# The block inverse of an RWKV-7 recurrence in one stretch of VectorE, and its 64-row products on quarters of the TensorE array

## The chip, the core and the metric

The kernel runs on one core of a Trainium2 chip. The metric is the device time of one launch in microseconds. Engines: PE is TensorE (matrix products, its weight loads are shown as PEld), DVE is VectorE, ACT is ScalarE, POOL is GpSimd, SP issues most DMAs. Each engine works its own instructions off in order; semaphores tie them together.

## What is computed

The kernel is one launch of three layers over 512 positions of width 1024: an attention layer, an RWKV-7 layer and a layer with two state-space branches, with the feed-forward parts. Only the recurrence of the RWKV-7 layer is touched. For each of 16 heads (64 channels) and both directions it computes, position after position,

```
sa    = state @ (-kk_t)
state = state * w_t + outer(sa, kk_t * a_t) + outer(v_t, k_t)
out_t = state @ r_t
```

then a group norm over each head, a bonus term, a gate, and the sum over the two directions. All of it is in 32-bit floats.

## The kernel before, in words

Positions are cut into 8 chunks of 64, and the 16 heads into 8 pairs of heads. In a chunk the recurrence is solved with matrix products: the scores of the chunk's keys against its keys give a strictly triangular 64x64 matrix for each head and direction, which has to be inverted (plus the identity); with the inverse, a chunk becomes one affine step of the 64x64 state. The two directions lie side by side: direction 0 on one half of the 128 partitions, direction 1 on the other.

Function `rwkv` does this with eleven generators, each a stream of work over the 8 pairs: `values` (the product that gives v), `front` and two `half` (keys, decays), `scores`, `inverse`, `early`, `merge`, `mid`, `chain` and `post`.

- `scores` (four groups of two chunks for a pair) makes the masked scores, tile `at`, and stores the 32x32 diagonal blocks to DRAM (`nd_s`). There are nine `at` buffers: by its condition a group waits until the chain has done the steps of the group nine places earlier.
- `inverse` (L1694) loads the diagonal blocks in another layout, 16x16 sub-blocks with one matrix in each partition, into X and, for direction 1, XL. XL has the pool tag `v1`, which a tile of `merge` has too, with one buffer. After the copy of XL into X (L1704) it runs 14 steps of two VectorE operations, a product into `xt` and a sum into X. Each needs the one before it, and after each stands a `yield`. Then it sets the diagonal (L1715) and stores X to DRAM (`xd_s`).
- `merge` (L1741) loads the 16x16 inverses (`yd`), transposes them into `zd`, and puts the 64x64 inverses together with 32x32 products on TensorE: tile `tt`.
- `early` (L1719) fills one partition half of the tiles `uv` (one for each direction) with v and clears the other half with a memset on POOL.
- `mid` (L1811) takes each group of two chunks through three sets of products. `ahead` copies `ar` through TensorE with the identity (four instructions in the profile) and multiplies `at` by `uv` (eight), twice. Then `tt` multiplies the result (`ax`), ACT copies it out: the first halves into `ta`, the others into the halves of `uv` that were zero. Then `ta` multiplies `at`, and DVE adds `ar` and the identity to make the transfer matrix `m`. `tas` are two fixed `ta` tiles, cleared once, in which each direction's half of the partitions is filled for its own slot; the other half stays zero, so that products over 128 rows give the 64-row result.
- `chain` (L1873) takes the state through the 8 chunks with `m` and writes `o`; `post` (L1913) normalises it and stores `y`.

The profile shows two instructions on TensorE for each such product of 32-bit floats. A product's place in the array follows from its operands: its rows from the partitions that it reads, its columns from the partitions that it writes. 128*64 in a row means 128 rows and 64 columns of the array.

The order of the instructions is written when the program is built, by `weave` (L36). Each generator yields the engine and the tiles that its next piece of work needs (or a condition); `weave` keeps a small model of engine times and takes the piece that can start first, by the time at which engine and operands are free, and among equals the one that became ready first. All instructions up to the generator's next `yield` are issued in one go, and each compute engine keeps that order.

Of the kernel before, what the change touches and what calls it, by code (L numbers as in the profile page):

```python
# [24 lines left out]
class Net:  # L25
# [1265 lines left out]
    def rwkv(self, g_pre, mu_p, mu_n, w_r, w_k, w_v, w_o, k_k, k_a, r_k, gn_w, gn_b, w0, w1, w2, a0, a1, a2,  # L1291
# [35 lines left out]
        with ExitStack() as c0:  # L1327
# [110 lines left out]
            with ExitStack() as c1:  # L1438
# [2 lines left out]
                arp, uvp, qp = P1("arp", 2), P1("uvp", 2), P1("qp", 4)  # L1441
                cw = ExitStack()
                self.weights(cw, 2, 2)
                vout = self.pool(cw, "vout")
                late = {}
                pm, pu = P1("pm", 5, space=PSUM), P1("pu", 3, space=PSUM)
                mk = sh.tile([128, 2, 128], F32, name="mk")
# [7 lines left out]
                TT(V, ident2, self.ident[:, 0:64], self.ident[:, 64:128], AD)  # L1455
                zeros = lambda nm, shape: [sh.tile([128] + shape, F32, name=f"{nm}{j}") for j in range(2)]

                tts, ss, tas = zeros("tt", [8, 2, 64]), zeros("ss", [2, 128]), zeros("ta", [2, 2, 2, 64])
                for j, t in enumerate(tts + ss + tas):
                    (V, G)[j % 2].memset(t, 0.0)  # L1460
                bank = lambda: pm.tile([128, 512], F32, name="mb", tag="mb")
                T2 = lambda tag, bufs=2: tp.tile([128, 520], F32, name="tmp", tag=tag, bufs=bufs)
# [44 lines left out]
                def values():  # L1507

                    ws = {}

                    def weight(j):
                        raw = self.wraw.tile([128, 1024], F32, name="raw", tag="raw")
                        nc.sync.dma_start(out=raw.rearrange("p (a b) -> p a b", b=128), in_=w_v[:, rows(j)].rearrange("(k p) c -> p k c", p=128))
                        hi, lo = (self.whl.tile([128, 1024], F32R, name=n, tag=n) for n in ("whi", "wlo"))
                        yield AC, raw
                        ACT(hi, raw, AF.Copy)
                        yield DV, hi
                        TT(V, lo, raw, hi.bitcast(F32), SU)
                        ws[j] = [t.rearrange("p (a b) -> p a b", b=128) for t in (hi, lo)]

                    yield from weight(0)
                    for j in range(KD):
                        if j + 1 < KD:
                            yield from weight(j + 1)
                        b = bank()
                        for k in range(KD):
                            if k % 2 == 0:
                                yield PE, *ws[j]
                            self.mm3(b, (ws[j][0][:, k, :], ws[j][1][:, k, :]), (xv[k][:, 0, :], xv[k][:, 1, :]), k == 0, k == KD - 1)
                        yield AC, b  # L1530
                        t = vout.tile([128, S], F32, name="vo", tag="vo")
                        ACT(t, b, AF.Copy)
                        nc.sync.dma_start(out=rkv_d[2, rows(j), :], in_=t)
                        done["values"] = j + 1
                    cv.close()
                    cw.close()
                    late.update(mp=P1("mp", 2), arp=P1("arl", 1), o=P1("ol", 1), qp=self.pool(c0, "qpl", 5, side="right"))
# [156 lines left out]
                def inverse(p, st):  # L1694

                    yield lambda: done["pre"] > p
                    XL = sh.tile([128, 16, 32], F32, name="XL", tag="v1")
                    for q in range(2):

                        for d in range(2):  # L1700
                            o = slice(64 * d + 32 * q, 64 * d + 32 * q + 32)
                            nc.sync.dma_start(out=flat((X, XL)[d][o])[:, :512 - 16 * q], in_=nd_d[p, 32 * d:32 * d + 32, 528 * q:512 + 512 * q])
                    yield DV, XL
                    V.tensor_copy(out=X[H(1), :, 0:16], in_=XL[H(1), :, 0:16].rearrange("p s t -> p t s"))  # L1704
                    yield DV, X
                    xt = sh.tile([128, 64], F32, name="xt_", tag="xt_")
                    for j in range(1, 15):
                        n = 15 - j
                        t = xt[:, :j * n].rearrange("p (i c) -> p i c", c=n)
                        TT(V, t, X[:, 0:j, j].unsqueeze(2).to_broadcast([128, j, n]),  # L1710
                           X[:, j, j + 1:16].unsqueeze(1).to_broadcast([128, j, n]), M)
                        yield DV, xt
                        TT(V, X[:, 0:j, j + 1:16], X[:, 0:j, j + 1:16], t, AD)
                        yield DV, X
                    V.memset(flat(X)[:, 0:512:33], 1.0)  # L1715
                    nc.sync.dma_start(out=xd_v[p], in_=flat(X))
                    done["inverse"] += 1

                def early(p, st):  # L1719
# [5 lines left out]
                    yield lambda: done["step"] >= 8 * (p - 1)  # L1725
                    uv = [uvp.tile([128, 8, 2, 64], F32, name=f"uv{d}", tag=f"uv{d}") for d in range(2)]
                    st["uv"] = uv
                    for d in range(2):
                        yield PO,
                        G.memset(uv[d][H(d)], 0.0)  # L1730
                    yield PE, v
                    b = bank().rearrange("p (c t) -> p c t", t=128)
                    for c in range(4):
# [77 lines left out]
                def mid(p, st):  # L1811
# [5 lines left out]
                    def ahead(i):  # L1817
                        b = bank().rearrange("p (j h e x) -> p j h e x", j=2, h=2, e=2)
                        at = st["q", i]
                        for j in range(2):  # L1820
                            cs = chunk_of(2 * i + j)
                            for d in range(2):
                                MM(b[H(d), j, :, 0, :], ar[d][:, cs[d], d, :], self.ident.rearrange("p (h x) -> p h x", h=2), True, True)
                            for hp in range(2):
                                for d in range(2):
                                    MM(b[H(d), j, hp, 1, :], at[:, j, hp, 2 * d, H(d)], uv[d][:, cs[d], hp, :], True, True)
                        return b

                    for i in range(4):
# [15 lines left out]
                                for d in range(2):  # L1845
                                    MM(b[H(d), j, hp, :], tt[H(d), 2 * i + j, hp, :], ax[H(d), 2 * j + hp], True, True)
                        yield AC, b
                        ta = tas[i % 2]
                        for d in range(2):
                            ACT(ta[H(d), d], b[H(d), :, :, 0:64], AF.Copy)  # L1850
                        yield AC, b
                        ACT(uv[0][H(0), 2 * i:2 * i + 2], b[H(0), :, :, 64:128], AF.Copy)
                        yield AC, b
                        ACT(uv[1][H(1), 6 - 2 * i:8 - 2 * i][:, ::-1], b[H(1), :, :, 64:128], AF.Copy)
                        yield PE, ta
                        b = bank().rearrange("p (j d x) -> p j d x", j=2, d=2)
                        for j in range(2):
                            for d in range(2):
                                for hp in range(2):
                                    MM(b[H(hp), j, d, :], ta[:, d, j, hp, :], lhs(at[:, j], d, hp), True, True)  # L1860
                        yield DV, b
                        m = mp.tile([128, 2, 2, 128], F32, name="m", tag="m", bufs=3)
                        for d in range(2):
                            cs = slice(6 - 2 * i, 8 - 2 * i) if d else slice(2 * i, 2 * i + 2)
                            r = ar[d][:, cs, 1 - d, :]
                            TT(V, m[:, :, d, H(d)], b[:, :, d, H(d)], r[:, ::-1] if d else r, AD)
                        i4 = lambda t: t.rearrange("p j d x -> p j (d x)")[:, :, 64:192].rearrange("p j (d x) -> p j d x", d=2)
                        TT(V, i4(m), i4(b), ident2.unsqueeze(1).unsqueeze(1).to_broadcast([128, 2, 2, 64]), AD)
                        st["m", i] = m
                        b = nx  # L1870
                    done["mid"] += 1
# [266 lines left out]
```

## Time and profile before

| | us |
|---|---|
| median of 3 runs | 2333.58 (2332.74 to 2334.99) |
| the profiled execution | 2329.99 |
| its span | 2328.2 |
| PE busy, in the span | 2135.0 (92%) |
| DVE busy | 1276.4 (55%) |
| ACT busy | 1077.6 (46%) |
| POOL busy | 85.3 (4%) |

Times in the rows below are in us from the start of the span, durations of a group in the timeline run from the first start to the last end, and means are in ns. `<-` in an operation's name stands between what it writes and what it reads; after an idle time it stands before the operation that ended the wait. The recurrence lies between about 820 and 1340 us.

### The profile page before, as it was taken

To read this page: it belongs to the slowest core of one execution; us is meant where nothing else is said; L and a number is where in the kernel's file an instruction comes from. 1 tells how busy PE (TensorE), PEld (TensorE's weight loads), DVE (VectorE), ACT (ScalarE), POOL (GpSimd) and SP (SyncE) were. 2 spreads that over 40 slices of the span, in tenths; PEclk is the share of its full clock that TensorE was granted. 3 is DMA by queue.
4 is the path that set the end of the run, shared out by engine and by line. 5 is a ranking of instruction groups with operands and counts; after the bars stand their busy time and mean duration, and the time that the engine had idled before them with its cause. 6 is when DMAs were issued, how large, how long until landed. Compare 5 with 4: busy or idle time off the path is not lost. (4 is left out here: it accounts for less than half of the span.)

```text
span 2328.2 us, 40334 instructions
## 1 busy us (share of the span) xinstructions
PE 2135.0 (92%) x16330; PEld 1719.8 (74%) x16330; DVE 1276.4 (55%) x2562; ACT 1077.6 (46%) x1950; POOL 85.3 (4%) x123
## 2 busy tenths in 40 slices
PE   7898999999968788888898689999999999999998
PEld 6777788888856666666676568887787877788877
DVE  4656542333388765667664255387645566633353
ACT  4555353342356554777766544333233444522232
POOL 0000000000000000011100100000000000000000
PEclk9999999999979987989999899999999988899999
DMA  5311233233224233222222343324334544233341
GB/s 173 104 55 54 71 110 92 90 100 100 91 71 121 91 99 80 61 61 57 52 55 46 105 133 109 91 90 144 111 111 142 143 126 119 54 95 90 107 145 55
DMA packets 321028, 221.52 MB, mean 95 GB/s; under 512 B 82414, under 2 KB 274442, under 8 KB 320842
## 3 DMA queue, kind: packets, MB, share of 16 engines
q1 hardware_dynamic: 319402, 213.70, 32.3%
q10 hardware_dynamic: 1440, 5.24, 0.7%
q8 instruction: 129, 2.11, 0.4%
q14 instruction: 57, 0.47, 0.1%
HBM read 187.62 MB, written 27.07 MB: 92 GB/s over the span
## 5 line engine op out<-in xcount | busy, mean ns | idle before, releaser
L160 ACT ACTIVATE whi<-raw 128x1024 fp32r<-128x1024 f32 x220 | 231.1, 1052 | 585.9 <-PE mm L223 297.3
L161 DVE TENSOR_TENSOR wlo<-raw,whi 128x1024 fp32r<-128x1024 f32 x220 | 266.5, 1214 | 368.0 <-ACT whi L160 365.4
L222 PE MATMUL mm<-uth,whi 128*128 128x512 f32 (+1 forms) x1088 | 412.9, 382 | 2.1 <-ACT uth L196 2.1
L223 PE MATMUL mm<-utl,whi 128*128 128x512 f32 (+1 forms) x1088 | 406.6, 374 | 5.5 <-DVE utl L197 5.5
L224 PE MATMUL mm<-uth,wlo 128*128 128x512 f32 (+1 forms) x1088 | 406.6, 374 | 0.0
L223 PEld LDWEIGHTS mm<-utl,whi 128*128 128x128 f32 x1088 | 209.0, 192 | 43.2 <-DVE utl L197 6.7
L222 PEld LDWEIGHTS mm<-uth,whi 128*128 128x128 f32 x1088 | 208.3, 192 | 41.0 <-ACT uth L196 3.5
L224 PEld LDWEIGHTS mm<-uth,wlo 128*128 128x128 f32 x1088 | 208.8, 192 | 37.3 <-issue 1.1
L224 PE MATMUL mm<-whi,hl 128*128 128x512 f32 x512 | 200.6, 394 | 0.0
L222 PE MATMUL mm<-whi,hh 128*128 128x512 f32 x512 | 200.5, 394 | 0.0
L223 PE MATMUL mm<-wlo,hh 128*128 128x512 f32 x512 | 199.9, 393 | 0.0
L224 PEld LDWEIGHTS mm<-whi,hl 128*128 128x128 f32 x512 | 96.3, 188 | 22.0 <-issue 0.2
L223 PEld LDWEIGHTS mm<-wlo,hh 128*128 128x128 f32 x512 | 96.3, 188 | 21.6
L222 PEld LDWEIGHTS mm<-whi,hh 128*128 128x128 f32 x512 | 96.3, 188 | 21.5 <-issue 0.4
L222 PE MATMUL mm<-whi,uth 128*128 128x512 f32 x224 | 88.6, 401 | 8.5 <-ACT whi L160 6.4
L224 PE MATMUL mm<-whi,utl 128*128 128x512 f32 x224 | 88.7, 399 | 0.0
L223 PE MATMUL mm<-wlo,uth 128*128 128x512 f32 x224 | 88.5, 398 | 0.0
L1301 ACT ACTIVATE ss<-cp,wc 64x64 f32<-64x64 f32 x224 | 69.1, 309 | 27.6 <-PE cp L1302 22.7
L282 DVE TENSOR_TENSOR acc<-mm,acc 128x512 f32<-128x512 f32 x48 | 33.0, 688 | 77.6 <-PE mm L224 77.6
L223 PE MATMUL mm<-mx,whi 128*128 128x512 f32 x160 | 66.0, 412 | 4.6 <-DVE mx L1289 4.4
L222 PE MATMUL mm<-mx,whi 128*128 128x512 f32 x160 | 62.1, 415 | 7.2 <-ACT mx L1288 6.0
L1299 DVE SCALAR_TENSOR_TENSOR mt<-u_pad,vcol,mt 128x512 f32<-128x512 f32 x96 | 66.8, 745 | 1.4 <-ACT mt L1301 1.3
(554 smaller groups left out, 3966.3 us busy)
## 6 DMA issues: line engine op xcount, KB each, us to landing
raw<-in_mlp_w_dram SPq DMA_DIRECT2D x128, 512.0 KB
raw<-in_w_in_dram SPq DMA_DIRECT2D x44, 512.0 KB
raw<-in_attn_w_in_dram SPq DMA_DIRECT2D x18, 512.0 KB
gbt<-in_norm_g_dram ACTq DMA_DIRECT2D x8, 512.0 KB
raw<-in_attn_w_out_dram SPq DMA_DIRECT2D x8, 512.0 KB
raw<-in_rk_w_k_dram SPq DMA_DIRECT2D x8, 512.0 KB
h_s<-h SPq DMA_DIRECT2D x8, 512.0 KB
raw<-in_rk_w_r_dram SPq DMA_DIRECT2D x8, 512.0 KB
```

The source lines that it names most:

```text
L160: nc.scalar.activation(out=hi[:, :n], in_=raw[:, :n], func=AF.Copy)
L161: nc.vector.tensor_tensor(out=lo[:, :n], in0=raw[:, :n], in1=hi[:, :n].bitcast(F32), op=ALU.subtract)
L222: mm(out, lhsT=lhs[0], rhs=rhs[0], start=start, stop=False)
L223: mm(out, lhsT=lhs[0], rhs=rhs[1], start=False, stop=False)
L224: mm(out, lhsT=lhs[1], rhs=rhs[0], start=False, stop=stop)
L282: nc.vector.tensor_tensor(out=a, in0=p, in1=a, op=ALU.add)
L1299: STT = lambda e, o, a, s, b, o0, o1: e.scalar_tensor_tensor(out=o, in0=a, scalar=s, in1=b, op0=o0, op1=o1)
L1301: ACT = lambda o, i, f, **k: nc.scalar.activation(out=o, in_=i, func=f, **k)
```

## The change

1. `inverse`: the two `yield`s in the loop go, so the 28 operations are issued in one go; XL has a tag, and so a buffer, of its own.
2. `early`: the memsets of `uv` go.
3. `mid`, in `ahead`: the product of `at` and `uv` reads only the 64 partitions of `uv` that hold v, rows `H(1 - d)`; the columns stay `H(d)`.
4. `mid`: `ta` is a tile from a pool with both directions' halves side by side in the partitions, filled by one ACT copy. The products of `ta` with `at` read the 64 partitions of a direction, `H(d)`, and write the 64 partitions of a head, `H(hp)`; the two directions write two banks, and the order of the loops is changed.
5. `mid`: `m` is made by four DVE additions of 128x128 elements, two for each bank, where there were two of 128x128 and one of 128x256.
6. `values`: its output tile comes from the tag `tmq` (three buffers, shared with others) where it had a pool of its own.

```diff
-                vout = self.pool(cw, "vout")
...
-                tts, ss, tas = zeros("tt", [8, 2, 64]), zeros("ss", [2, 128]), zeros("ta", [2, 2, 2, 64])
-                for j, t in enumerate(tts + ss + tas):
+                tts, ss = zeros("tt", [8, 2, 64]), zeros("ss", [2, 128])
+                for j, t in enumerate(tts + ss):
...
-                        t = vout.tile([128, S], F32, name="vo", tag="vo")
+                        t = TQ()
...
-                    XL = sh.tile([128, 16, 32], F32, name="XL", tag="v1")
+                    XL = sh.tile([128, 16, 32], F32, name="XL", tag="XL")
...
                         TT(V, t, X[:, 0:j, j].unsqueeze(2).to_broadcast([128, j, n]),
                            X[:, j, j + 1:16].unsqueeze(1).to_broadcast([128, j, n]), M)
-                        yield DV, xt
                         TT(V, X[:, 0:j, j + 1:16], X[:, 0:j, j + 1:16], t, AD)
-                        yield DV, X
...
-                    for d in range(2):
-                        yield PO,
-                        G.memset(uv[d][H(d)], 0.0)
...
-                                    MM(b[H(d), j, hp, 1, :], at[:, j, hp, 2 * d, H(d)], uv[d][:, cs[d], hp, :], True, True)
+                                    MM(b[H(d), j, hp, 1, :], at[H(1 - d), j, hp, 2 * d, H(d)], uv[d][H(1 - d), cs[d], hp, :], True, True)
...
-                        ta = tas[i % 2]
-                        for d in range(2):
-                            ACT(ta[H(d), d], b[H(d), :, :, 0:64], AF.Copy)
+                        ta = mp.tile([128, 2, 2, 64], F32, name="ta", tag="ta")
+                        ACT(ta, b[:, :, :, 0:64], AF.Copy)
...
                         yield PE, ta
-                        b = bank().rearrange("p (j d x) -> p j d x", j=2, d=2)
+
+                        bs = [bank()[:, :256].rearrange("p (j x) -> p j x", j=2) for _ in range(2)]
                         for j in range(2):
-                            for d in range(2):
-                                for hp in range(2):
-                                    MM(b[H(hp), j, d, :], ta[:, d, j, hp, :], lhs(at[:, j], d, hp), True, True)
-                        yield DV, b
+                            for hp in range(2):
+                                for d in range(2):
+                                    MM(bs[d][H(hp), j, :], ta[H(d), j, hp, :], lhs(at[:, j], d, hp)[H(d)], True, True)
                         m = mp.tile([128, 2, 2, 128], F32, name="m", tag="m", bufs=3)
                         for d in range(2):
+                            yield DV, bs[d]
                             cs = slice(6 - 2 * i, 8 - 2 * i) if d else slice(2 * i, 2 * i + 2)
                             r = ar[d][:, cs, 1 - d, :]
-                            TT(V, m[:, :, d, H(d)], b[:, :, d, H(d)], r[:, ::-1] if d else r, AD)
-                        i4 = lambda t: t.rearrange("p j d x -> p j (d x)")[:, :, 64:192].rearrange("p j (d x) -> p j d x", d=2)
-                        TT(V, i4(m), i4(b), ident2.unsqueeze(1).unsqueeze(1).to_broadcast([128, 2, 2, 64]), AD)
+                            TT(V, m[:, :, d, H(d)], bs[d][:, :, H(d)], r[:, ::-1] if d else r, AD)
+                            TT(V, m[:, :, d, H(1 - d)], bs[d][:, :, H(1 - d)], ident2.unsqueeze(1).to_broadcast([128, 2, 64]), AD)
```

## Rows read from the trace of the kernel before

**Rows 1.** Table by stage: stretch, its length, busy us (count) by engine, granted clock, DMA.
```profile
1083.00:1136.00 53.00, 45.35 (x989) 34.48 (x985) 36.79 (x102) 40.17 (x103) 6.77 (x6) 1.00 0.24 57
930.00:1320.00 390.00, 339.20 (x7029) 265.28 (x7025) 235.15 (x665) 280.32 (x731) 41.47 (x34) 0.94 0.23 53
```

**Rows 2.** Timeline of one loop: start, us, engine, line, operation, shape, count.
```profile
1064.08 1.16 PE L1302 MATMUL mb<-ar,bk 64*128 64x128 f32 x16
...
1126.79 0.70 DVE L1751 STREAM_TRANSPOSE zd<-yd 128x512 f32<-128x512 f32 x1
...
1159.35 0.41 DVE L1298 TENSOR_TENSOR m<-mb,ident 128x256 f32<-128x256 f32 x1
...
1170.93 1.16 PE L1302 MATMUL mb<-ar,bk 64*128 64x128 f32 x16
```

**Rows 3.** Timeline of SP's queue before the inverse of the fifth pair.
```profile
1090.39 0.78 SPq L1702 DMA_DIRECT2D X<-nd_s  x2
...
1093.61 1.27 SPq L1680 DMA_DIRECT2D nd_s<-at  x3
1094.98 0.84 SPq L1702 DMA_DIRECT2D XL<-nd_s  x2
```

**Rows 4.** Timeline of PE: the last reads of the `v1` buffer in `merge`.
```profile
1088.57 1.52 PE L1302 MATMUL mb<-yz,v 32*32 32x32 f32 x64
```

**Rows 5.** Timeline of DVE: first and last operation of the fifth pair's inverse.
```profile
1097.53 0.38 DVE L1704 COPY X<-XL 64x256 f32<-64x256 f32 x1 [3.28 <-DMA XL<-nd_s]
...
1117.34 0.07 DVE L1715 MEMSET X<- 128x16 f32 x1
```

**Rows 6.** Busy time of DVE in that stretch: all, then operations on X alone.
```profile
1097.50:1117.50 20.00, 18.93 (x59) 1.00 0.17 51
...
1097.50:1117.50 20.00, 5.97 (x30) 1.00 0.17 51
```

**Rows 7.** Tile X, products of four pairs: ns min/median/max, first and last start.
```profile
L1298 DVE TENSOR_TENSOR xt__7438<-X x14: 175/200/217, 940.1 to 956.4; 128x14 f32<-128x14 f32 x2, 128x26 f32<-128x26 f32 x2, 128x36 f32<-128x36 f32 x2, 128x44 f32<-128x44 f32 x2
...
L1298 DVE TENSOR_TENSOR xt__9100<-X x14: 164/200/243, 1045.4 to 1063.8; 128x14 f32<-128x14 f32 x2, 128x26 f32<-128x26 f32 x2, 128x36 f32<-128x36 f32 x2, 128x44 f32<-128x44 f32 x2
...
L1298 DVE TENSOR_TENSOR xt__10862<-X x14: 164/206/241, 1150.7 to 1171.6; 128x14 f32<-128x14 f32 x2, 128x26 f32<-128x26 f32 x2, 128x36 f32<-128x36 f32 x2, 128x44 f32<-128x44 f32 x2
...
L1298 DVE TENSOR_TENSOR xt__12438<-X x14: 165/203/217, 1249.8 to 1261.4; 128x14 f32<-128x14 f32 x2, 128x26 f32<-128x26 f32 x2, 128x36 f32<-128x36 f32 x2, 128x44 f32<-128x44 f32 x2
```

**Rows 8.** Timeline of PE: groups of products of several shapes.
```profile
1062.03 0.40 PE L1302 MATMUL mb<-uv,at 128*64 128x64 f32 x8
1062.26 0.39 PE L1302 MATMUL mb<-ident,ar 128*64 128x128 f32 x4
...
1063.06 1.09 PE L1302 MATMUL mb<-ax,tt 64*64 64x128 f32 x16 [0.18 <-ACT ax L1301]
...
1067.28 0.69 PE L1302 MATMUL cp<-uv,at 128*64 128x64 f32 x16
1067.89 0.71 PE L1302 MATMUL cp<-ss,m 128*128 128x128 f32 x4
...
1072.78 1.09 PE L1302 MATMUL mb<-at,ta 128*64 128x128 f32 x16
...
1086.01 0.75 PE L1302 MATMUL mb<-yz,at 32*32 32x32 f32 x64
1086.70 0.79 PE L1302 MATMUL cp<-ss,m 128*128 128x128 f32 x4
```

**Rows 9.** Groups between 930 and 1320 us: shapes, count | busy us, mean ns | idle before.
```profile
L1301 ACT ACTIVATE ta<-mb 64x256 f32<-64x256 f32 x64 | 24.1, 377 | 30.2 <-PE mb L1302 29.3
...
L1301 ACT ACTIVATE at<-mb 128x256 f32<-128x256 f32 x50 | 16.4, 381 | 19.0 <-PE mb L1687 18.5
...
L1298 DVE TENSOR_TENSOR m<-mb,ar 128x128 f32<-128x128 f32 x64 | 15.4, 281 | 25.0 <-PE mb L1302 24.4
...
L1298 DVE TENSOR_TENSOR m<-mb,ident 128x256 f32<-128x256 f32 x32 | 13.2, 414 | 0.0
```

## The prediction

> **What bounds the kernel now.** I read the page's busy shares first: TensorE (PE) is busy nearly everywhere, so the question is the one stage that the change touches, the recurrence. The table by stage comes next [rows 1]: between 930 and 1320 us PE is busy 339.20 of 390 us at a mean granted clock of 0.94, so it stands idle for 50.8 us. In one undisturbed head pair (1083 to 1136, clock 1.00) PE is busy 45.35 of 53, VectorE (DVE) 36.79, ScalarE (ACT) 40.17. No engine is full. A stage in which nothing is full waits for a loop of dependencies, so I followed one pair through the timeline.
>
> The loop [rows 2]: the second `scores` group of the fifth pair starts at 1064.08. Its `at` tiles go through DRAM into the inverse, the inverse through DRAM into `merge` (transpose of `zd` at 1126.79), `merge` lets `mid` make the first transfer matrix `m` (1159.35), and two `chain` steps on that `m` give back the `at` buffer that the same `scores` group two pairs later needs: 1170.93. That is 106.85 us for two pairs, 53.4 for one, which is the pace of the stage. Two such loops run side by side, one over the first, third, fifth and seventh pair, one over the others. So time is won here only on the loop, and no more than PE's idle time, as long as PE's own work stays.
>
> Two stretches of the loop are waiting, not work. The inverse runs from the copy at 1097.53 to the memset at 1117.34 [rows 5], 19.9 us. In 20 us around it DVE is busy 18.93, of which only 5.97 belong to the inverse [rows 6]: since the inverse yields after each operation, all other DVE work that is ready is put before its next one. And the load of `XL` shares a buffer with `merge`'s `v1`: the last reads of that buffer by PE run from 1088.57 to 1090.09 [rows 4], the X loads leave at 1090.39, but the XL loads only at 1094.98, behind three `nd_s` stores on SP's queue [rows 3].
>
> **The change part by part.** All sums are against the profiled execution, 2329.99 us with a span of 2328.2 and 1.8 around it; the median of the runs shown, 2333.58, is 3.6 above it, and the final number is moved to that.
>
> *Inverse in one block.* It removes 28 yields, no instruction. The products alone now spread over 16.3, 18.4, 20.9 and 11.6 us in the second, fourth, sixth and eighth pair, first start to last start [rows 7]. In one block: 28 operations inside 5.97 us of busy time [rows 6], plus the short gaps between dependent ones; bounds 5.5 (busy time less the copy) and 9 us, I take 6.2, near the busy row, because nothing but the inverse's own order is left. Gain along that loop, which holds the last pair: 10.1 + 12.2 + 14.7 + 5.4 = 42.4 us. What pays for it: 18.93 − 5.97 = 13.0 us of other DVE work in that window must wait up to 6 us.
>
> *XL with a buffer of its own.* XL's loads can leave with X's: 1094.98 − (1090.39 + 0.78) = 3.8 us in this pair [rows 3]. Bounds 0 (another pair's stores may stand elsewhere on SP's queue) and 3.8 in each of the loop's three later passes; I take 2.5, so 7.5 us.
>
> *`ta` by one copy.* Two ACT copies of 64x256 (377 ns each) become one of 128x256 (381 ns for that form) [rows 9]: 32 groups × 0.373 = 12 us off ACT. On the loop lie about three of these groups per pass (the one that makes the first `m` and the two before the next `scores`), some ten in all: 3.7 us.
>
> *`m` by four additions.* Two of 281 ns and one of 414 become four of 281 [rows 9]: +0.148 us, 4.7 in all on DVE, 1.5 on the loop. Each half starts after its own bank.
>
> *The product with `ta` in quarters.* Sixteen instructions (eight products), now on tiles of 128*64, two at a time: 1.09 us from first start to last end [rows 8]. Afterwards both row halves and both column halves are used, so four can run together. The price with four comes from the 32*32 products of `merge`, which use two row groups and two column groups each: 64 of them from 1086.01 to 1086.70, 0.69 us, 0.53 without the change of shape (below). One 32-column instruction needs about 29 ns on its tile, half of what a 64-column one needs (eight of these, two at a time, in 0.23 us), so 64 × 29 / 0.53 us gives 3.5 at a time [rows 8]. Two at a time `ax,tt` needs 1.02 us [rows 2, 8], 0.86 without the change of shape; four at a time 0.43. Gain 0.43 × 32 = 14 us of PE, on the loop 4.3. Bounds: 0 (still two at a time) and 0.54 a group.
>
> *`ahead` on half of the rows.* Its products with `uv` use tiles 64*64 after the change, while the copies of `ar` between them stay 128*64. These four groups follow each other today without a change of shape: eight instructions from 1062.03 to 1062.26, 0.23 us. Sixteen of the same size after a change of shape take 1067.28 to 1067.89, 0.61, that is 0.15 more than twice 0.23 [rows 8]. The change makes three such places in each `ahead`: 0.45 × 32 = +14.4 us of PE, +4.5 on the loop. Bounds 0 and 0.2 a place. Nothing runs faster for it: two products at a time before, and two after, since the row half and the column half change together.
>
> The Trainium skill, TensorEngine Tiling (Array Packing), section Tiling Modes, says that changing the tiling mode drains the engine; the rows above agree, with 0.15 us a place. By that rule alone this edit is a loss of 14 us. The same page, section Restrictions and Gotchas, says that different row tiles cannot use one PSUM bank at the same time. `ahead` keeps one bank for both row halves, so by that rule its pairs would run one by one and cost another 0.23 × 2 × 32 = 15 us. The trace does not bear this out: `ax,tt` has row tiles 0 and 64 in one bank and takes 1.09 us, as the column-tiled product does [rows 8].
>
> *The rest.* The two memsets of `uv` go from POOL, which is idle for almost the whole stage [rows 1]; nothing on the loop waits for them: 0, at most their few us where `early` is late. `values` takes its output tile from the three `tmq` tiles instead of one of its own: 0, between a gain and a loss of about one eviction a block, ahead of the steady part.
>
> *Sum.* On the loop −42.4 − 7.5 − 3.7 − 4.3 + 1.5 + 4.5 = −51.9 us. On PE −14 + 14.4, nothing: its 339 us stay, and the 50.8 us idle are all there is to win. Latency would allow 52 and PE 51; both cannot be had whole, since PE executes in order and what stops waiting for the inverse meets DVE's block, ACT or the next pair. Between 0 and 51 I take a little over half, 27 us: 2303 for the profiled execution, 2307 for the median of runs.
>
> **The rivals.**
> 1. *The whole idle time goes.* The two loops pull apart enough that PE runs through: −48, 2285. For it: latency falls by as much. Against: PE would have to be busy without a break at a full clock, and 0.94 was granted.
> 2. *PE sets the pace already.* Then the inverse was hidden, and PE's sum decides: −14 + 14.4, so 2334. For it: PE 87% busy. Against: PE still has 7.65 us idle in the undisturbed pair at full clock, and the loop explains its pace.
> 3. *The products with `ta` stay two at a time* while `ahead` pays its places: PE has 14 us more, about 11 of which show at its share: 2318.
> 4. *The block holds up DVE* (slower). In each window 13.0 us of other DVE work, with the `m` and `at` operands of the other loop in it, is put back by up to 6 us. If those operands, not the inverse, are late for PE, seven blocks at 1.3 to 6 us cost 9 to 42, less the little won elsewhere: about +16, 2350. It decides from the point where a block delays the other loop by more than it shortens its own, half of 13 us. Against: these operands are a few 0.3 to 0.7 us operations, and DVE has 16 of 53 us free in a pair.
>
> **How the numbers follow.** Forecast 0.55 (its own range 2290 to 2322), rival 1 0.13, rival 2 0.13, rival 3 0.10, rival 4 0.09. About 0.2% (4.7 us) is what a measurement of this kernel can tell from no change. Faster: forecast, 1, 3 and a third of 2: 0.82. Slower: 4 and a little of 2: 0.11. Same: 0.07. The range 2283 to 2336 leaves out the far end of 1, and 4.
>
> **What would show it.** Right: copy to memset of X under 8 us in the middle pairs, XL's loads right behind X's, the loop of two pairs under 100 us, PE idle near 25 us in the recurrence, the `ta` product about 0.6 us, three pauses in PE's weight loads inside each `ahead`. Wrong: a loop that is still 107 us with a short inverse (then the time went to `merge` or `mid`), `m` additions that start more than 2 us after their product because DVE is in the block, or a granted clock clearly under 0.94 because PE's gaps became longer.

## The result, and the profile after

The change made the kernel slower: 2376.82 us (median of 4 runs, 2374.59 to 2379.56) against 2334.28 for the kernel before on the same chip, a ratio of 1.0182, 95% interval 1.0169 to 1.0196. The forecast was 2307 with a range up to 2336. The profiled execution has a span of 2372.8 us, 44.6 more than before.

The table by stage shows where, in the columns of [rows 1] (stretch, its length, busy us and count of PE, PEld, DVE, ACT, POOL, granted clock, DMA):

```profile
930.00:1320.00 390.00, 310.72 (x6174) 232.65 (x6171) 231.12 (x666) 233.64 (x602) 27.95 (x21) 0.85 0.21 48
```

The same stretch had PE busy for 339.20 us and a clock of 0.94 [rows 1]. PE's idle time went from 50.8 us to 79.3, where the forecast wanted about 25, and the granted clock fell with it. (The stretch is the same in time, not in work: the slower kernel gets less far in it.) What PE waited for is one row of the table of waits between 930 and 1320 us (who waited, for whom, us in all, times, longest), here of before and then of after:

```profile
PE mb L1948 <- DVE o L1298: 0.7, 2, 0.5
```

```profile
PE mb L1941 <- DVE o L1298: 28.2, 9, 6.7
```

These are the transposes in `post`, waiting until DVE has normalised the output `o`. That wait grew by 27.5 us, of the 28.5 us by which PE's idle time grew; PE's other idle time hardly changed in sum (50.1 and 51.1 us). The last transposes of `post` end at 1386.4 us, 51 later than before (1335.1).

The parts did what the prediction said of them, one by one. The inverse, in the tile view (ns min/median/max, first to last start), takes 6.2 us from its first product to its last in a middle pair, against up to 20.9 [rows 7]:

```profile
L1298 DVE TENSOR_TENSOR xt__10971<-X x14: 167/204/219, 1191.6 to 1197.8; 128x14 f32<-128x14 f32 x2, 128x26 f32<-128x26 f32 x2, 128x36 f32<-128x36 f32 x2, 128x44 f32<-128x44 f32 x2
```

XL's loads now leave beside X's (timeline of SP's queue), where three stores stood between them [rows 3]:

```profile
1179.55 0.78 SPq L1701 DMA_DIRECT2D XL<-nd_s  x2
1180.53 0.77 SPq L1701 DMA_DIRECT2D X<-nd_s  x2
```

The product with `ta` takes 0.67 us on quarters, first start to last end, against 1.09 [rows 8]. Inside `ahead` a group of eight products with `uv` is followed by the copy of `ar` after 0.37 us instead of 0.23 [rows 8], so 0.14 us for a change of shape (timeline of PE):

```profile
1171.21 0.45 PE L1302 MATMUL mb<-uv,at 64*64 64x64 f32 x8
1171.58 0.44 PE L1302 MATMUL mb<-ident,ar 128*64 128x128 f32 x4
...
1178.82 0.67 PE L1302 MATMUL mb<-at,ta 64*64 64x128 f32 x16
```

The one copy of `ta` takes 383 ns, and each of the four additions for `m` about 285 (groups between 930 and 1320 us), as [rows 9] said:

```profile
L1298 DVE TENSOR_TENSOR m<-mb,ar 128x128 f32<-128x128 f32 x54 | 15.4, 285 | 44.8 <-PE mb L1302 44.6
L1298 DVE TENSOR_TENSOR m<-mb,ident 128x128 f32<-128x128 f32 x54 | 15.2, 282 | 0.0
...
L1301 ACT ACTIVATE ta<-mb 128x256 f32<-128x256 f32 x27 | 10.3, 383 | 21.4 <-PE mb L1302 21.2
```

So every predicted local gain is there, and the time is lost elsewhere. DVE's timeline around the block of the sixth pair shows the place: the block stands in the middle of another stream's work.

```profile
1187.74 0.68 DVE L1930 TENSOR_REDUCE rg<-tmp 128x8 f32<-128x512 f32 x1
...
1189.24 0.39 DVE L1703 COPY X<-XL 64x256 f32<-64x256 f32 x1
1189.66 1.29 DVE L1298 TENSOR_TENSOR at<-mb,mk 128x512 f32<-128x512 f32 x2
...
1190.94 0.68 DVE L1930 TENSOR_REDUCE rg<-tmp 128x8 f32<-128x512 f32 x1
...
1191.61 0.17 DVE L1298 TENSOR_TENSOR xt__10971<-X 128x14 f32<-128x14 f32 x1
...
1197.98 0.18 DVE L1298 TENSOR_TENSOR X<-X,xt__10971 128x14 f32<-128x14 f32 x1
...
1198.12 0.07 DVE L1712 MEMSET X<- 128x16 f32 x1
1198.16 0.16 DVE L1300 TENSOR_SCALAR rg<-rg 128x16 f32<-128x16 f32 x1
...
1203.20 0.69 DVE L1298 TENSOR_TENSOR o<-o,rg 128x512 f32<-128x512 f32 x1
```

`rg` belongs to `post` of the fourth pair, whose chain has just ended. Its second sum starts at 1190.94; its next step, the scaling of `rg` by 1/64, needs only that sum, but starts at 1198.16, behind the whole block. Then follow `post`'s power on POOL (another power, `rn`, is ahead of it by now), the product with `o`, and the transposes on PE; and only then the chain of the next pair, which writes into the same `o` (timelines of POOL and of PE):

```profile
1198.32 1.64 POOL L1298 TENSOR_TENSOR rn<-rn,mhalf 128x8 f32<-128x8 f32 x1 [10.96 <-DVE rg L1300]
1199.92 2.90 POOL L1298 TENSOR_TENSOR rg<-rg,mhalf 128x16 f32<-128x16 f32 x1
```

```profile
1204.03 0.63 PE L1941 MATMUL mb<-ident,o 128*128 128x128 f32 x4 [1.93 <-DVE o L1298]
1207.82 1.09 PE L1941 MATMUL mb<-ident,o 128*128 128x128 f32 x4 [3.17 <-DVE o L1298]
...
1211.86 0.69 PE L1302 MATMUL cp<-uv,at 128*64 128x64 f32 x16
```

The last row is the first product of the next chain. In the kernel before the same sum and scaling stand 0.76 us apart, with a single operation of the inverse between them (DVE's timeline of before):

```profile
1097.93 0.69 DVE L1937 TENSOR_REDUCE rg<-tmp 128x8 f32<-128x512 f32 x1
1098.54 0.16 DVE L1655 COPY bns<-mb 128x8 f32<-128x8 f32 x1
1098.61 0.16 DVE L1298 TENSOR_TENSOR xt__9981<-X 128x14 f32<-128x14 f32 x1
1098.69 0.17 DVE L1300 TENSOR_SCALAR rg<-rg 128x16 f32<-128x16 f32 x1
```

The order is `weave`'s: by its rule it takes what can start first, and when the sum has been issued, the scaling must wait for its result, while the inverse can start at once. Into that small gap it put one 0.16 us operation before, and 28 operations now, because nothing yields between them.

This is a second loop, which the prediction had not followed: chain of a pair, `post` of that pair, chain of the next pair. `o` has one buffer (pool `ol`), and the chain yields on `done["post"] > p - 1`. Before, from the fourth pair: chain starts 1108.6, last piece of `o` at 1143.4, `post`'s last transposes done 1163.5, next chain 1164.3: 55.7 us. This is PE's timeline of before, the first and the last row being the two chains' first products:

```profile
1108.56 0.69 PE L1302 MATMUL cp<-uv,at 128*64 128x64 f32 x16
...
1162.89 0.63 PE L1948 MATMUL mb<-ident,o 128*128 128x128 f32 x4 [0.24 <-DVE o L1298]
...
1164.31 0.69 PE L1302 MATMUL cp<-uv,at 128*64 128x64 f32 x16
```

After, the same pair: 1150.0, 1180.9, 1208.9, 1211.9: 61.9 us. From the second chain's start to the seventh's (five pairs) it is 262.2 us before, 52.4 a pair, which is the pace of the loop through the inverse too, and 294.9 after.

Two loops of nearly one length ran beside each other, then. The block shortens one and lengthens the other, and the longer one sets the pace. That the first did get shorter shows too: the first `m` of the fifth pair is now ready at 1180, 32 us before its chain starts. In the kernel before it was ready at 1159.8, 4.5 us ahead of its chain: even there it lay finished while the chain waited for `post`, so the loop through the inverse, as the prediction timed it, held a wait for the other loop.

### The profile page after: what moved, and what is told of

Same layout as the page of the kernel before. It is cut to its first block, busy times and chain, and to the rows that moved or that the text cites. A ratio compares the mean times of both kernels' runs of the same rounds, so it can differ in the third digit from the quotient of the medians.

```text
span 2372.8 us, 40329 instructions
## 1 busy us (share of the span) xinstructions
PE 2139.1 (90%) x16330; PEld 1708.8 (72%) x16330; DVE 1284.4 (54%) x2593; ACT 1065.2 (45%) x1918; POOL 70.1 (3%) x106
## 5 line engine op out<-in xcount | busy, mean ns | idle before, releaser
L1298 DVE TENSOR_TENSOR at<-mb,mk 128x512 f32<-128x512 f32 x64 | 41.2, 683 | 54.4 <-PE mb L1302 54.3
```

Of the source, the lines that this page charges most:

```text
L1298: TT = lambda e, o, a, b, op: e.tensor_tensor(out=o, in0=a, in1=b, op=op)
```

## The experiments

Two theories were held against each other from the start. A: the loop through `post` sets the pace, and the block costs what it puts between `post`'s operations on DVE. B: the loss comes from PE, from the products on half of the rows, or from the buffers (`tmq`). Ratios are to the kernel before, run on the same chip, with 95% intervals.

### The parts

**All yields back, in the kernel after.**
```diff
+                        yield DV, xt
                         TT(V, X[:, 0:j, j + 1:16], X[:, 0:j, j + 1:16], t, AD)
+                        yield DV, X
```


> The changed kernel with the two yields put back into the inverse's loop; all else as changed. Theory A (block): the block of 28 operations holds VectorE while post's small scaling of the group norm's sums waits; in the changed trace it starts 7.2 us after the sums in the fourth pair (1190.9 to 1198.2) where it took 0.8 before, and post stands between a pair's chain and the next pair's. So without the block the time falls by some 30 to 40 us, to 2337 to 2347, and post takes about 18 us again from the chain's last output. Rival B (TensorE: half-row products and changes of shape, or the granted clock): it stays above 2365. Rival V (the output tile of values): some 7 us of the loss remain.


Measured: 2339.41 us, 1.0029 (1.0009 to 1.0049). Without the block, 1.5% of the 1.8% is gone. What is left of the change is still a small loss, not the 10 us gain that the other terms of the sum had.

**The block alone, in the kernel before** (the two yields taken out, nothing else).


> The kernel before with only the two yields taken out. Theory A: slower by 25 to 45 us, 2360 to 2379, with post at 25 to 28 us in the first five pairs. Rival B: no change, 2330 to 2338, or faster by the shorter inverse.


Measured: 2386.59, 1.0230 (1.0211 to 1.0249): the block alone is worse than the whole change, and 8 us above A's range. DVE's timeline shows the same picture, sum and scaling 8.4 us apart, with the end of the block beside the scaling:
```profile
1187.06 0.69 DVE L1935 TENSOR_REDUCE rg<-tmp 128x8 f32<-128x512 f32 x1
...
1195.47 0.15 DVE L1300 TENSOR_SCALAR rg<-rg 128x16 f32<-128x16 f32 x1
1195.50 0.07 DVE L1713 MEMSET X<- 128x16 f32 x1
```

**The middle part alone, in the kernel before** (`mid` and `early` of the kernel after, changes 2 in `early` and 3 to 5).


> The kernel before with only the parts of mid and early: half-row products, ta by one copy, four additions, no memset. Theory A: within 10 us of 2334, since TensorE loses 0.45 us a group in ahead and wins 0.44 in the product with ta. Rival B: 2350 or more.


Measured: 2340.34, 1.0023 (1.0002 to 1.0043).

**Quarters for the `ta` product only, in the kernel before**: one copy of `ta`, products in quarters, four additions; `ahead` on 128 rows and the memsets kept.


> The kernel before with the product of ta in quarters, one copy and four additions, but ahead on all 128 rows as before (memset kept), so without the changes of shape inside ahead. TensorE wins 0.44 us in each of 32 groups, 14 us, and loses nothing. If TensorE sets the pace: 2318 to 2322. If the rings do: 2326 to 2338. Against the run with half rows in ahead (2340) it shows what the changes of shape cost, up to 14 us.


Measured: 2324.54, 0.9963 (0.9947 to 0.9978): faster than before, and between the two ranges that were expected, so it doesn't tell whether PE or the loops set the pace. With the run above this splits the middle part: quarters −0.4%, half rows in `ahead` (the memsets go with them) +0.6%.

**The same with XL's own buffer and `values` on `tmq`**, so the whole change without block and half-row `ahead`.


> The changed kernel with the yields put back and with ahead on all 128 rows again (memset kept): what is left of the change is XL's own buffer, values' shared output tile, the product of ta in quarters. Beside the run without the first two (2324.5) it shows what these two are worth: by the prediction 7.5 us less, 2312 to 2320; by theory A, in which the ring through post sets the pace, nothing or the 3 us that values' shared tile costs, 2320 to 2330.


Measured: 2319.90, 0.9950 (0.9933 to 0.9968), the best of all kernels run, at the upper end of the range by the prediction and 0.1 us under A's. Against the run above the intervals overlap, so what XL's buffer adds (3 us by these two ratios) is not resolved.

**A pool of its own for `values` again, in the kernel after.**


> The changed kernel with the own pool of values' output tile put back. Rival V: the last value block is copied out at 921.6 us in the changed trace, 910.4 before, and the first chain starts 6.8 us later, since post holds two of the three shared tiles from 859 us on; with the pool back the time falls by 7 to 11 us, to 2366 to 2370. Theory A alone, and B: within 3 us of 2377.


Measured: 2373.81, 1.0194 (1.0160 to 1.0228). The rival's range was missed, and A's by 0.2 us. The ratio is that of the whole change (1.0182), so no part of `tmq` in the loss is seen.

### The loop through `post`

**The scaling kept with the sum, in the kernel after**: one yield less in `post`, so that the scaling is issued with the sum and no block comes between them.
```diff
-                    yield DV, rn
                     TS(V, rn, rn, 1.0 / 64, 64e-5, M, AD)
```


> The changed kernel with post's scaling issued in one go with the second sum, so that the block can't come between these two; the block stays whole. Theory A: the 7 us between sum and scaling go, but the block then stands beside POOL's power (2.9 us) and holds back the multiplication of o behind it by up to 4 us: 2350 to 2362. If the wait of the scaling were only a sign of something else, no change: 2374 to 2380.


Measured: 2360.73, 1.0126 (1.0107 to 1.0145), inside A's range. Taking that one wait away, with the block still whole, gives some 13 us back (by the ratios, 1.0182 to 1.0126). It did not give all, and the timeline says why: the block now stands before `post`'s next operation on DVE, the product with `o`, which follows the end of the block:
```profile
1176.30 0.67 DVE L1930 TENSOR_REDUCE rg<-tmp 128x8 f32<-128x512 f32 x1
1177.01 0.17 DVE L1300 TENSOR_SCALAR rg<-rg 128x16 f32<-128x16 f32 x1
...
1183.67 0.07 DVE L1712 MEMSET X<- 128x16 f32 x1
1183.71 0.68 DVE L1298 TENSOR_TENSOR o<-o,rg 128x512 f32<-128x512 f32 x1
```

**Two `o` tiles, in the kernel after.**
```diff
-                    yield lambda: done["post"] > p - 1 and late
+                    yield lambda: done["post"] > p - 2 and late
```
(and `ol` with two buffers)


> The changed kernel with two o tiles, so that a pair's chain waits for the post of the pair before the last one, not of the last one. Theory A says that the pace is the ring chain, post, next chain, and that the block only costs because it stands in post. With the ring opened the block should cost little: the transfer matrices m of the next pair are made 30 us before its chain starts in the changed trace, so the time falls to 2300 to 2335. Rival (the block delays the masks and m operands for TensorE, wherever they are): it stays above 2360.


Measured: 2353.86, 1.0099 (1.0082 to 1.0116). A miss for A's number, though it gives back 0.8%. The chain does start before `post` is through (the first product of the fourth pair's chain at 1130.40, transposes of the third pair's `o` from 1136.98 on):
```profile
1130.40 1.12 PE L1302 MATMUL cp<-uv,at 128*64 128x64 f32 x16
...
1136.98 0.66 PE L1941 MATMUL mb<-ident,o 128*128 128x128 f32 x4
```
But its steps then take some 51 us instead of 32, the five pairs 293.7 us (294.9 without this edit); what is won is won at the start, where the second pair's chain no longer waits for the first pair's `post` and begins 28 us earlier. What holds the pace there is not settled.

**Two `o` tiles, in the kernel before.**


> The kernel before with two o tiles. Theory A: the ring sets the pace there too (53 us a pair, of which post takes 18), but m of the next pair is made only 5 us before its chain starts, so the gain ends there: 2295 to 2330. Rival (the loop by scores, inverse and merge sets the pace, as the prediction had it): no change, 2330 to 2338.


Measured: 2338.92, 1.0031 (1.0011 to 1.0051): no gain. A's range was missed; the rival's "no change" ended 1 us below it. This fits two loops of nearly equal length: with one opened, the other keeps the pace. The trace shows the hand-over: in the second to the fifth pair the chain now starts within 0.3 us of its first `m`, where it came 4.5 to 5.9 us behind it before, and its steps take 45.7 us instead of 34.7.

**`post` ahead of all others** (`weave` gives `post` a lead of 5 us), in the kernel after and in the kernel before.
```diff
-[(each(f), 0.0) for f in (
+[(each(f), 5.0 if f is post else 0.0) for f in (
```


> The changed kernel, block whole, but in the writing of the order post is preferred by 5 us over all other streams: its scaling and its multiplications stand ahead of the block though they become ready a little later. Theory A (the block costs because it stands inside post, on the ring chain, post, next chain): post goes back to 18 us or less and the time to 2315 to 2345. If the block harms in many places, 2360 or more.

> The kernel before with the same preference for post. Two rings of equal length (one through post, one through scores, inverse, merge and mid): shortening one alone gives little, 2322 to 2336. If the ring through post alone sets the pace: 2310 or less.


Measured: 2444.67, 1.0475 (1.0451 to 1.0499), and 2429.68, 1.0421 (1.0400 to 1.0443). Both missed by far, and both teach the same: `post` fell to 10.6 us, but from the third pair on the inverse's copy of X came 28 to 31 us after the pair's last mask instead of some 11, and from chain to chain it took 64 to 75 us (the first five). The first `m` of the second to the fifth pair is ready within 2 us of its chain's start, so the loop through the inverse sets the pace here. Favouring either loop at the other's cost loses.

**The block held back until `post` is through**, in the kernel after and in the kernel before with the `ta` quarters.
```diff
+                    yield lambda: done["post"] >= p - 1
                     xt = sh.tile([128, 64], F32, name="xt_", tag="xt_")
```


> The changed kernel, block whole, but it is issued only after the post of the pair two before has been issued, so that it can't stand inside that post; it begins some 10 to 20 us later. Theory A: post goes back to 18 to 22 us, the ring through inverse and merge stays short enough since m is made 30 us too early in the changed trace: 2325 to 2350. If most of the block's harm lies elsewhere: 2360 or more.

> The kernel before with the product of ta in quarters, and with the block, issued only after the post of the pair two before. Theory A: no worse than the same kernel without the block (2324.5), 2305 to 2330. If the block harms wherever it stands: 2340 or more.


Measured: 2353.38, 1.0097 (1.0075 to 1.0118), and 2352.03, 1.0095 (1.0077 to 1.0113). The first ended 3 us above A's range; the second lies in the rival's range (the block harms wherever it stands). `post` is down to 13.6 us, below its 17.7 before. DVE's timeline of the first shows where the block stands now: in the chain's beginning, between the first and the second transfer matrix.
```profile
1165.46 0.28 DVE L1298 TENSOR_TENSOR m<-mb,ar 128x128 f32<-128x128 f32 x1
...
1171.46 0.16 DVE L1298 TENSOR_TENSOR xt__11004<-X 128x14 f32<-128x14 f32 x1
...
1177.96 0.07 DVE L1713 MEMSET X<- 128x16 f32 x1
...
1180.38 0.28 DVE L1298 TENSOR_TENSOR m<-mb,ar 128x128 f32<-128x128 f32 x1
```
The product for that second `m` is done on PE at 1174.7, and its addition comes 5.7 us later, behind the block. But the chain doesn't wait for it (timeline of PE):
```profile
1171.17 0.69 PE L1302 MATMUL cp<-uv,at 128*64 128x64 f32 x16
...
1173.72 1.00 PE L1302 MATMUL mb<-at,ta 64*64 64x128 f32 x16
1177.90 2.07 PE L1302 MATMUL mb<-lg,wg 128*128 128x512 f32 x2 [3.19 <-ACT ax L1301]
1179.77 1.06 PE L1302 MATMUL cp<-ss,m 128*128 128x128 f32 x4
...
1187.47 0.71 PE L1302 MATMUL cp<-ss,m 128*128 128x128 f32 x4
```
The step at 1179.77 takes the first `m`, ready since 1166.3; the second is first used at 1187.47, 6.2 us after its last addition. What is late is the first step, 8.6 us after the chain's start (3.3 before, in the same pair): it stands on PE behind a product of `post`, `lg,wg`, before which PE was idle for 3.19 us until ACT's copy `ax` ended. That copy empties one of the five PSUM banks `mb`; the other four, by the two timelines, hold results that DVE reads only behind the block (1177.93 to 1181.26). So the next victim seems to be the supply of free banks; no run tried this. The chain's steps take 41.0 us here, 34.7 before (means of the second to the fifth pair).

### How long a piece may be

The kernel after with a yield in the middle of the loop (`if j == 7: yield DV, X`), after each step, and after every fourth step.


> The changed kernel with one yield in the loop, after its seventh step: two blocks of 14 operations, about 3.3 us each, in place of one of 6.6. Theory A: a ready operation waits for one half at most, so about half of the loss is left, 2350 to 2362. If any block does the same harm, 2370 or more; if only single operations can be passed, as with all yields, 2339 is its lower end.

> The kernel after with one yield after each step of the inverse (product and addition stay together, so DVE's block is 2 operations instead of 28). Theory A (what costs is the length of the piece that can stand between post's second sum and its scaling): a piece of two operations is about 0.5 us, so the sum-to-scaling gap stays under 1.5 us, post takes 12 to 21 us as before, and the time is that with all yields, 2336 to 2346 (ratio 1.001 to 1.006). Theory B (what costs is that any inverse of this shape is put ahead, whatever the length of its pieces, as the run with two halves may say): still 2360 to 2377.

> The kernel after with a yield after every fourth step of the inverse (pieces of up to 8 operations, about 2 us). Theory A, length of the piece: one piece of about 2 us stands between post's sum and its scaling where 8 us stood, so about a quarter of the loss beside the shape changes: 2344 to 2356 (ratio 1.005 to 1.010). Theory B, the inverse is put ahead whatever the length of its pieces: 2365 to 2377.

| DVE operations in a piece | ratio | `post`: last `o` to second sum | sum to scaling | scaling to power | rest | all |
|---|---|---|---|---|---|---|
| 1 (all yields) | 1.0029 | 4.6 | 2.1 | 0.2 | 12.0 | 18.9 |
| 2 (each step) | 1.0026 (1.0008 to 1.0043), 2337.19 us | 3.9 | 1.8 | 0.2 | 11.1 | 17.0 |
| 8 (every fourth) | 1.0135 (1.0099 to 1.0172), 2361.79 us | 9.7 | 2.7 | 1.5 | 10.5 | 24.4 |
| 14 (halves) | 1.0181 (1.0160 to 1.0203), 2373.30 us | 9.7 | 4.2 | 1.5 | 9.9 | 25.3 |
| 28 (the change) | 1.0182 | 8.7 | 7.6 | 1.0 | 9.2 | 26.6 |

(The columns of `post` are us from the timelines, means of the second to the fifth pair.) Two-operation pieces cost nothing beside all yields. A's expectation for each step was met. The halves ended in the rival's range (any block does the same harm), and every fourth step between the two ranges. The wait that A names does grow from two operations on, 1.8, 2.7, 4.2, 7.6 us. The total does not follow it, since shorter pieces slip in at more places: with halves or every fourth step a piece stands before the product with `o` as well (2.2 and 2.5 us between the power's end and that product, 0.6 with the whole block), and in front the sums are late too. DVE's timeline with a yield after every fourth step shows both: a row of `bk` and `ar` operations of a later pair, here between 1167.95 and 1174.74, stands ahead of the sums, and eight operations of the inverse stand before the scaling.
```profile
1167.95 0.42 DVE L1298 TENSOR_TENSOR bk<-tmp 128x256 f32<-128x256 f32 x1
...
1174.74 0.69 DVE L1298 TENSOR_TENSOR tmp<-r,tmp 128x512 f32<-128x512 f32 x1
1175.35 0.68 DVE L1932 TENSOR_REDUCE rg<-tmp 128x8 f32<-128x512 f32 x1
...
1178.57 0.68 DVE L1932 TENSOR_REDUCE rg<-tmp 128x8 f32<-128x512 f32 x1
...
1180.79 0.20 DVE L1298 TENSOR_TENSOR X<-X,xt__10971 128x44 f32<-128x44 f32 x1
...
1180.98 0.16 DVE L1300 TENSOR_SCALAR rg<-rg 128x16 f32<-128x16 f32 x1
```
The first sum starts 6.8 us after the last `o` here, 3.8 before (means as in the table). The whole block has that row of operations in front too (first sum 6.8 us after the last `o` in the third to the fifth pair). So A's one wait is a part of the cause: sum to scaling is 6.6 of the 8.9 us by which `post` grew per pair under the whole block, 1.7 of 6.7 with every fourth step, and taking it away gave back 0.6 of the block's 1.5%. The rest is the order into which the other generators fall once the inverse moves. That this order is an outcome of the pieces' length, rather than of something that goes with it, was not tried by itself and stays open.

## Why the prediction was wrong

*The failed step is "The loop".* It took the pace, 53.4 us a pair, from a loop through the inverse, found that the loop explains it, and stopped: "So time is won here only on the loop". The pace had a second loop of nearly the same length (52.4 us a pair), chain to `post` to chain, whose rows (last `o`, `post`'s sums and transposes, the next chain) were in the trace of before. The hint lay in the loop that it followed: `m` ready at 1159.8, its chain only at 1164.3, 0.8 us behind the end of `post`. In the kernel after the second loop takes 59.0 us a pair. Shortening one of two such loops wins nothing by itself: two `o` tiles in the kernel before, which open the other loop, gave 1.0031.

*"Inverse in one block", −42.4 us on the loop.* The latency did fall as stated (6.2 us). Its effect was +1.5% (1.0182 against 1.0029), about 36 us with the other sign. The text named the price, 13.0 us of other DVE work put back by up to 6 us, but not which operation it was and who waits for it. One of `post`'s 0.16 us operations, the scaling, accounts for some 13 of these 36 us; the rest was found only in part.

*Rival 4* (the block holds up DVE) had the sign, the mechanism and, by the range of 9 to 42 us, nearly the size, at a chance of 0.09 and with the wrong victims. `m` was not late in the kernel after: it was ready 32 us early, and even where the block is held back until `post` is through, the chain has each `m` at least 4.9 us before its use (second to fifth pair). Its point of decision, "more than it shortens its own", is not the right one either: the chain already waited for `post` in the kernel before, so a delay in `post` moves the chain at once.

*"DVE has 16 of 53 us free in a pair"* was used against rival 4. It doesn't bear on it. DVE was busy for 231 us of the 390 in the kernel after, no more than before (235); the loss is order, not load.

*`ahead` on half of the rows, +14.4 us on PE, +4.5 on the loop.* The price of a place was right, 0.14 us against 0.15. What it does to the time was not: with and without it (the memsets go with it), 1.0023 against 0.9963, and 1.0029 against 0.9950, so +0.6 to +0.8%, 14 to 18 us. The PE sum, not the share on the loop, was the better estimate. The Trainium skill, TensorEngine Tiling (Array Packing), section Tiling Modes, whose rule (a change of tiling mode drains the engine) the prediction gave, spoke against this edit, and the trace agrees. By the rule of the same page of the Trainium skill on banks (section Restrictions and Gotchas) the 64*64 groups in one bank would run one by one; eight instructions and a change of shape in 0.37 us, where the same eight took 0.23 without either, leave no room for that: row tiles in one bank did run together.

*The product with `ta`, −14 us on PE.* Size right: 1.09 us became 0.67 (predicted 0.6 or so). With the copy and the additions it gave −0.37% (8.6 us), against −6.5 us as the sum of its terms on the loop (−3.7, +1.5, −4.3). This part alone was right in sign and nearly in size; whether it came by the loop or by PE's sum, the runs don't tell.

*XL, −7.5 us.* Its loads do follow X's directly; the gain, about 3 us, is not resolved. *`values` and the memsets, 0*: the run with the pool back agrees for `values`; the memsets were not tried by themselves.

*The clock.* "Clearly under 0.94 because PE's gaps became longer" was named as a sign of a wrong forecast, and came: 0.85. How much of the loss is the lower clock and how much the gaps was not separated; of the gaps, nearly all that was added is the wait for `o`.

*Still open:* why the block costs about 0.7% more than with yields when it stands behind `post` (one place, where PE seems to lack a free bank, was read in the trace and not tried); why two `o` tiles keep the pace at 58.7 us a pair in the kernel after; and the row of `bk` and `ar` operations in front of `post`.

## What to carry to other kernels

A loop whose length equals the pace proves that it may set the pace, not that it alone does: before you count a gain on it, look for other loops of that length, and start from each buffer with one copy (who waits until it is free?). A finished operand that lies unused on your loop, here `m` for 4.5 us, is a hint that another loop is the longer one. Making many short operations of an in-order engine one uninterruptible block lends that engine to one stream: name the shortest operation of every other stream that can become ready just behind its start, because what it costs is the wait of whoever needs that one. Here pairs of operations cost nothing, blocks of eight 1.1% more; and a change that is a bundle of gains and losses is worth taking apart, since the quarters and the buffers alone are 0.5% faster than before.

## What the runs showed of the hardware that was not expected

The granted clock differed between kernels in which PE was about equally busy. The two kernels with half-row products in `ahead` and all yields had 0.90 and 0.89 (PE busy 344.98 and 343.56 of 390 us); before, and the two kernels with `ahead` on 128 rows, had 0.94, 0.92 and 0.92 (339.20, 333.10 and 336.25). That the half rows are the reason is not shown: with a yield after each step they had 0.91 (337.78), and the kernel before with two `o` tiles, on 128 rows, had 0.91 too (330.04). Each figure is from one execution. Here are the rows of the kernel after with its yields, and then of the fastest kernel (the stretch as in [rows 1]):

```profile
930.00:1320.00 390.00, 344.98 (x6985) 255.08 (x6982) 236.34 (x689) 258.70 (x679) 29.17 (x22) 0.90 0.22 51
```

```profile
930.00:1320.00 390.00, 336.25 (x7140) 261.29 (x7138) 239.84 (x700) 272.07 (x720) 41.16 (x35) 0.92 0.24 57
```

A lower clock makes the same products longer: in the kernel after eight `uv` products take 0.45 us from 1171.21 on, at a granted clock of 1.00 (2.4 GHz), and 0.69 us from 1191.66 on, at 0.50 (1.2 GHz). That may be why the loss by the half rows showed in full; no run tells these apart. The stretch behind the recurrence, which the change doesn't touch, is 993 us in the profile of before and 986 in that of after (from `post`'s last transposes to the end of the span), so the recurrence lost 51 us, of which the span shows 44.6.
